# Gate and up of two feed-forwards: part of the K tiles as 2x2 block products with seven multiplications

## The chip, the cores and the metric

The kernel runs on one core of a Trainium2 chip. Its engines work side by side, each through its own queue of instructions in order: TensorE (PE, matrix products into PSUM; the loading of its stationary operand is shown as PEld), VectorE (DVE), ScalarE (ACT), GpSimd (POOL) and SyncE (SP, which issues the loads). They wait for each other through semaphores. The metric is the device time of one execution in microseconds. The kernel before takes 2145.21 us, the median of three runs (2145.0 to 2145.99). By 0.2% of it, 4.3 us, a difference between two kernels can just be told from none.

## The reference

One layer of a Conformer-like encoder on 256 tokens of 2048 features, all in float32. It opens and closes with a feed-forward whose hidden width is 5632:

```python
def swiglu_ffn(h, w_in, w_out):
    gate, up = jnp.split(h @ w_in, 2, axis=-1)
    return (jax.nn.silu(gate) * up) @ w_out

x = x + 0.5 * swiglu_ffn(rms_norm(x, ffn1_norm), ffn1_w_in, ffn1_w_out)
...   # token mixing (convolution and spatial gating), then cross-attention into 256 memory tokens
x = x + 0.5 * swiglu_ffn(rms_norm(x, ffn2_norm), ffn2_w_in, ffn2_w_out)
return rms_norm(x, final_norm)
```

The change is in the two feed-forwards, above all in `h @ w_in`.

## The kernel before

All products are made from two-part numbers. A float32 operand is split into a high part that TensorE takes as it is and the low rest; a product is high x high, high x low and low x high, three matmuls. The weights are split on the way in: SP loads 512 KB into one of four `raw` buffers (L104), ScalarE casts it to the high part (L107), VectorE subtracts that from the raw values (L108) and so gives the low part. High and low part lie in one of three `hl` buffers.

Gate and up (`swiglu_in`) go through 11 groups of 512 hidden columns. In a group the 16 K tiles of 128 features come one after the other; a `raw` tile holds 512 gate and 512 up columns of one K tile. `by_two` makes the products: for each half of the tokens (128 of them, the stationary operand `x_hl`) and for gate and up, three 128x512 matmuls (L273, L274, L277), 12 for a K tile and 192 for a group, summed in four banks of PSUM (`acc`, from a pool of six). Then ScalarE makes silu of gate out of PSUM (L289), VectorE multiplies it by up (L290), and the result `h` waits in one of two buffers. It has tokens on its partitions; the next product needs features there. So `turn` transposes it on TensorE, four 128x128 blocks to a turning (L303), into one of two more banks (`aux`), from where ScalarE and VectorE split it into `hA` or `hB` (L115, L116). The two turnings of a group are made inside the next group, after its fourth and sixth K tile.

The output product (`gemm_n`, L166 to L168) runs over 44 hidden tiles for each of four blocks of 512 columns, two hidden tiles to a load and a step of 12 matmuls.

Work that belongs to other things is put in small parts beside the products: `put` enters parts with a cost, `beside` takes them out by a budget at each step. In the first feed-forward these are four loads of mem and their squares, with a budget of 1.4 in each step; in the second they are the 32 turnings of x (L790), with a budget of 0.4. The order of each engine's queue within all this is set by the tile framework's scheduler. The large operands of two parts (`x_hl`, `hA`, `m_hl`, `y_hl`, `o_hl`) share two big buffers that change hands; a new owner waits until the last reader of the old one is done.

Of the kernel before, what the change touches and what calls it, by code (L numbers as in the profile page):

```python
# [11 lines left out]
F32 = mybir.dt.float32  # L12
# [5 lines left out]
P = 128  # L18
D = 2048
T = 256  # L20
# [15 lines left out]

PV_SIZES = [
# [24 lines left out]
def layer(ctx: ExitStack, tc: tile.TileContext, a: dict):  # L62
# [4 lines left out]
    big = ctx.enter_context(tc.tile_pool(name="big", bufs=2))  # L67
# [170 lines left out]
    def gained_tile(norm):  # L238

        return big.tile([P, KD, 2, T], F32R, name="x_hl", tag="S")  # L240
# [26 lines left out]
    def by_two(acc, x, hi, lo, first, last):  # L267

        for t in range(2):
            s = slice(t * P, (t + 1) * P)  # L270
            for g in range(2):
                c = slice(g * G, (g + 1) * G)
                nc.tensor.matmul(acc[t][g], lhsT=x[:, 0, s], rhs=hi[:, c], start=first, stop=False)  # L273
                nc.tensor.matmul(acc[t][g], lhsT=x[:, 0, s], rhs=lo[:, c], start=False, stop=False)  # L274
            for g in range(2):
                c = slice(g * G, (g + 1) * G)
                nc.tensor.matmul(acc[t][g], lhsT=x[:, 1, s], rhs=hi[:, c], start=False, stop=last)  # L277

    def token_accs():
        return [[ps.tile([P, 2, 256], F32, name="acc").rearrange("p a b -> p (a b)") for _ in range(2)] for _ in range(2)]  # L280

    def swiglu_in(pool, x_hl, root, w_in, hA, hB, first, per):

        turns = []

        def gated(acc, r):
            h = pool.tile([P, 2, G], F32, name="h", bufs=2)
            for t in range(2):
                nc.scalar.activation(out=h[:, t], in_=acc[t][0], func=AF.Silu, scale=r[:, t:t + 1])  # L289
                nc.vector.scalar_tensor_tensor(  # L290
                    out=h[:, t], in0=acc[t][1], scalar=r[:, t:t + 1], in1=h[:, t], op0=ALU.mult, op1=ALU.mult
                )
            return h

        def turn(j, h, half):
            def go():
                f = 4 * j + 2 * half
                dst = hA[:, f:f + 2] if f < KD else hB[:, f - KD:f - KD + 2]
                tp = pa.tile([P, 2, T], F32, name="aux")
                for k in range(2):  # L300
                    for t in range(2):
                        c = slice((2 * half + k) * P, (2 * half + k + 1) * P)
                        nc.tensor.transpose(out=tp[:, k, t * P:(t + 1) * P], in_=h[:, t, c], identity=ident)  # L303
                split(dst[:, :, 0], dst[:, :, 1], tp)
            return go

        r = None
        for j in range(NG):
            if j == 0 and first is not None:
                acc = first()  # L310
            else:
                acc = token_accs()
                for k in range(KD):
                    hi, lo = weights(w_in[j, :, k:k + 1], 1, 2 * G)
                    by_two(acc, x_hl[:, k], hi[:, 0], lo[:, 0], k == 0, k == KD - 1)
                    if k in (3, 5) and turns:
                        turns.pop(0)()
                    beside(per)
            if r is None:
                r = root()  # L320
            h = gated(acc, r)
            turns += [turn(j, h, half) for half in range(2)]
        return turns

    def h_of(hA, hB):
        return lambda k: hA[:, k] if k < KD else hB[:, k - KD]


    x_hl = gained_tile("ffn1_norm")
    ss = st.tile([P, T], F32, name="ss", bufs=2)  # L330

# [604 lines left out]
```

## Time and profile before

| | |
|---|---|
| median of three runs | 2145.21 us |
| the profiled execution | 2147.76 us, its span 2146.0 us |
| PE busy | 2124.5 us, 99% of the span, 9944 matmuls |
| VectorE busy | 1284.9 us, 60% |
| ScalarE busy | 1005.5 us, 47% |
| DMA | 190 GB/s from HBM on average, median landing time of a gate and up load 3.7 us |
| granted TensorE clock | 0.999 |

The busy time of PE is modelled from the pipelined matmuls: a 128x512 matmul is shown with some 0.39 us, though the next one starts earlier. What a matmul costs is therefore read from the spacing of the work that hangs on it, not from its length. The same holds, to a lesser degree, for VectorE, whose instructions overlap a little when they stand back to back. A busy share is an average over stages: the first and last feed-forward, two thirds of the time, are unlike the middle, where VectorE is at 70 to 90% in places.

### The profile page before, as it was taken

How to read it: one execution, taken by the hardware profiler on the slowest of the kernel's cores; microseconds unless marked ns; L12 is line 12 of the kernel's file. 1: busy time of each engine (PE TensorE's matmuls, PEld its weight loads, DVE VectorE, ACT ScalarE, POOL GpSimd, SP SyncE). 2: the span in 40 equal slices, each digit the busy share in tenths (PEclk: the TensorE clock that was granted, in tenths of full speed). 3: DMA queues.
4: the chain of work that ended last, by engine and by line, in shares of the span. 5: the costliest groups of instructions: out<-in, count | busy, mean ns of one | idle time of the engine just before them, and what ended most of it. 6: DMA issues, size and time to landing. Idle time of an engine off the chain costs nothing.

```text
span 2146.0 us, 26016 instructions
## 1 busy us (share of the span) xinstructions
PE 2124.5 (99%) x9944; PEld 1770.8 (83%) x9944; DVE 1284.9 (60%) x1627; ACT 1005.5 (47%) x1234; POOL 13.3 (1%) x23
## 2 busy tenths in 40 slices
PE   8999999999999999999999999999999999999998
PEld 6788888888888888888888888888888888888886
DVE  4655445545554589889877666766644455444444
ACT  5544444444444454544665454544444444444443
POOL 0000000000000000000000000000000000000000
PEclk9999999999999999999999999999999999999999
DMA  7666666666666676656565543666666666666664
GB/s 271 223 189 192 188 189 192 187 188 189 193 188 194 195 245 199 187 177 186 175 199 187 185 158 115 201 193 188 187 189 193 188 186 192 190 208 194 195 191 154
DMA packets 113598, 409.80 MB, mean 191 GB/s; under 512 B 12737, under 2 KB 12865, under 8 KB 113345
## 3 DMA queue, kind: packets, MB, share of 16 engines
q1 hardware_dynamic: 113184, 407.35, 62.2%
q8 instruction: 78, 1.28, 0.2%
q10 hardware_dynamic: 288, 0.79, 0.1%
q14 instruction: 48, 0.39, 0.0%
HBM read 405.99 MB, written 2.10 MB: 190 GB/s over the span
## 4 chain that ended last, share of the span: by engine, by line
PE 95%; DMA 2%; DVE 1%; ACT 1%; issue 1%; SPq 0%; DVEq 0%; ACTq 0%
PE acc L274 14%; PE acc L277 14%; PE acc L273 14%; PE acc L167 12%; PE acc L168 12%; PE acc L166 12%; PE acc L120 8%; PE acc L121 4%; PE acc L857 1%; PE acc L859 1%; PE acc L858 1%; DMA raw<-in_x 1%; PE aux L303 1%; DMA raw<-in_memT 1%; PE aux L257 0%
## 5 line engine op out<-in xcount | busy, mean ns | idle before, releaser
L108 DVE TENSOR_TENSOR hl<-raw,hl 128x1024 fp32r<-128x1024 f32 x751 | 915.6, 1222 | 783.8 <-ACT hl L107 782.4
L107 ACT CAST hl<-raw 128x1024 fp32r<-128x1024 f32 x751 | 784.8, 1049 | 1007.7 <-PE acc L277 505.6
L274 PE MATMUL acc<-hl,x_hl 128*128 128x512 f32 x1408 | 446.9, 392 | 0.6 <-DVE hl L108 0.5
L277 PE MATMUL acc<-hl,x_hl 128*128 128x512 f32 x1408 | 441.3, 390 | 0.0
L273 PE MATMUL acc<-hl,x_hl 128*128 128x512 f32 x1408 | 395.4, 393 | 10.0 <-ACT hl L107 8.4
L273 PEld LDWEIGHTS acc<-hl,x_hl 128*128 128x128 f32 x1408 | 261.5, 188 | 63.5 <-ACT hl L107 9.7
L277 PEld LDWEIGHTS acc<-hl,x_hl 128*128 128x128 f32 x1408 | 264.8, 188 | 55.7
L274 PEld LDWEIGHTS acc<-hl,x_hl 128*128 128x128 f32 x1408 | 263.0, 188 | 55.4 <-DVE hl L108 2.1
L167 PE MATMUL acc<-hl,hB 128*128 128x512 f32 x392 | 152.7, 389 | 0.0
L168 PE MATMUL acc<-hl,hB 128*128 128x512 f32 x392 | 152.6, 389 | 0.0
L166 PE MATMUL acc<-hl,hB 128*128 128x512 f32 x392 | 136.7, 389 | 0.0
L167 PE MATMUL acc<-hl,x_hl 128*128 128x512 f32 x256 | 100.6, 393 | 0.8 <-DVE hl L108 0.8
L167 PE MATMUL acc<-hl,m_hl 128*128 128x512 f32 x256 | 100.4, 392 | 0.0
L168 PE MATMUL acc<-hl,m_hl 128*128 128x512 f32 x256 | 100.2, 392 | 0.0
L168 PE MATMUL acc<-hl,x_hl 128*128 128x512 f32 x256 | 99.8, 390 | 0.0
L166 PE MATMUL acc<-hl,m_hl 128*128 128x512 f32 x256 | 91.3, 393 | 0.0
L120 PE MATMUL acc<-x_hl,hl 128*128 128x512 f32 x256 | 90.6, 396 | 0.0
L120 PE MATMUL acc<-y_hl,hl 128*128 128x512 f32 x256 | 90.5, 399 | 0.0
L166 PE MATMUL acc<-hl,x_hl 128*128 128x512 f32 x256 | 90.2, 392 | 0.0
L120 PE MATMUL acc<-o_hl,hl 128*128 128x512 f32 x256 | 89.2, 393 | 0.0
L167 PE MATMUL acc<-hl,hA 128*128 128x512 f32 x224 | 87.8, 392 | 0.0
L168 PE MATMUL acc<-hl,hA 128*128 128x512 f32 x224 | 87.3, 390 | 0.0
(208 smaller groups left out, 2243.6 us busy)
## 6 DMA issues: line engine op xcount, KB each, us to landing
raw<-in_ffn_w_in SPq DMA_DIRECT2D x352, 512.0 KB, 3.7
raw<-in_ffn_w_out SPq DMA_DIRECT2D x176, 512.0 KB, 3.7
raw<-in_w_mix_vg SPq DMA_DIRECT2D x32, 512.0 KB, 4.5
raw<-in_w_k SPq DMA_DIRECT2D x32, 512.0 KB, 3.8
raw<-in_w_v SPq DMA_DIRECT2D x32, 512.0 KB, 4.2
raw<-in_w_mix_out SPq DMA_DIRECT2D x32, 512.0 KB, 4.5
raw<-in_w_q SPq DMA_DIRECT2D x32, 512.0 KB, 4.3
raw<-in_w_o SPq DMA_DIRECT2D x29, 512.0 KB, 4.5
```

What stands on the lines that cost most here:

```text
L107: nc.scalar.copy(out=hl[:, 0, :size], in_=raw[:, :size])
L108: newest[0] = nc.vector.tensor_tensor(out=hl[:, 1, :size], in0=raw[:, :size], in1=hl[:, 0, :size].bitcast(F32), op=ALU.subtract)
L120: nc.tensor.matmul(acc, lhsT=w_hi, rhs=x_hl, start=first, stop=False, skip_group_check=True)
L121: nc.tensor.matmul(acc[:, 0], lhsT=w_lo, rhs=x_hl[:, 0], start=False, stop=last, skip_group_check=True)
L166: nc.tensor.matmul(acc[t], lhsT=x[:, 0, s], rhs=hi[:, k], start=k0 + k == 0, stop=False)
L167: nc.tensor.matmul(acc[t], lhsT=x[:, 0, s], rhs=lo[:, k], start=False, stop=False)
L168: nc.tensor.matmul(acc[t], lhsT=x[:, 1, s], rhs=hi[:, k], start=False, stop=k0 + k == nk - 1)
L273: nc.tensor.matmul(acc[t][g], lhsT=x[:, 0, s], rhs=hi[:, c], start=first, stop=False)
L274: nc.tensor.matmul(acc[t][g], lhsT=x[:, 0, s], rhs=lo[:, c], start=False, stop=False)
L277: nc.tensor.matmul(acc[t][g], lhsT=x[:, 1, s], rhs=hi[:, c], start=False, stop=last)
L303: nc.tensor.transpose(out=tp[:, k, t * P:(t + 1) * P], in_=h[:, t, c], identity=ident)
L857: nc.tensor.matmul(acc[t], lhsT=x[:, 0], rhs=hi[:, k], start=first, stop=False)
```

## The change

For some pairs of K tiles the 24 matmuls become 21. A pair is taken as a 2x2 block product: the left matrix has the two halves of the tokens as block rows and the two K tiles as block columns, the right one has the two K tiles as block rows and gate and up as block columns. Such a product can be made with seven block multiplications instead of eight, if sums and differences of blocks are multiplied and the results are added afterwards (`seven`). A string says for each of the 8 pairs whether it is done with seven products (S) or as before with eight (C): SCSCSCCC in the first feed-forward, SCCSCCCC in the second. The first group of each feed-forward is done wholly as before.

What comes with it:

- The sums of the left blocks (`sides`, four forms of 128x128 for each S pair) are made once, in the first group, and kept split in `ring`.
- The sums of the right blocks are made by VectorE for each S pair of each group: four instructions of 512 columns (L370, L371, L376, L383). Two of them overwrite part of the raw tile. With them an S pair has three and a half 1024 wide tiles to split instead of two.
- A group uses all eight banks, the two of `aux` included. After its last S pair, ScalarE copies one bank (L418) and VectorE makes four sums (L419 to L422); at the end of the group four more (L432), then silu and the product (L397, L399) from SBUF.
- Since `aux` is taken, h is kept for all 11 groups, and its turnings stand in the last group (four of 22) and in the first output product (18, one after each step).
- The split weights have five buffers instead of three: `hl` and two in `ring`. There are now three big buffers S0, S1, S2; in the middle part `kT` and `vv` lie in one of them.
- The loads of mem and their squares move from the second group to the second and later output products of the first feed-forward, with a budget of 0.8 per step; the 32 turnings of x move into the first group of the second feed-forward, with a budget of 1.3.
- At the end, one `held` buffer is left of four for the last weights; the others come from `hl`.

The right operand is laid out in DRAM so that for even K tiles up stands before gate. That is part of the arrays' preparation. The diff, cut to its core:

```diff
+PATTERNS = ("SCSCSCCC", "SCCSCCCC")
...
-    big = ctx.enter_context(tc.tile_pool(name="big", bufs=2))
+    big = ctx.enter_context(tc.tile_pool(name="big", bufs=1))
...
+    def three(acc, x, hi, lo, first, last):
+
+        nc.tensor.matmul(acc, lhsT=x[0], rhs=hi, start=first, stop=False)
+        nc.tensor.matmul(acc, lhsT=x[0], rhs=lo, start=False, stop=False)
+        nc.tensor.matmul(acc, lhsT=x[1], rhs=hi, start=False, stop=last)
...
+        def parts(self, raw, n=1024, last=False):
+
+            i = self.at % 5
+            self.at += 1
+            hl = whl.tile([P, 2, 1024], F32R, name="hl") if last or i < 3 else self.ring[i - 3]
+            nc.scalar.copy(out=hl[:, 0, :n], in_=raw[:, :n])
+            newest[0] = nc.vector.tensor_tensor(
+                out=hl[:, 1, :n], in0=raw[:, :n], in1=hl[:, 0, :n].bitcast(F32), op=ALU.subtract
+            )
+            return hl
...
+        def seven(self, j, p, b, first, last):
+
+            k = 2 * p
+            one, two = self.raw(j, k), self.raw(j, k + 1)
+            sums = self.sums[self.spairs.index(p) % 2]
+            lo, hi = slice(0, G), slice(G, 2 * G)
+            nc.vector.tensor_tensor(out=sums[:, lo], in0=one[:, hi], in1=one[:, lo], op=ALU.subtract)
+            nc.vector.tensor_tensor(out=sums[:, hi], in0=two[:, hi], in1=one[:, lo], op=ALU.subtract)
+            w = self.parts(sums)
+            form = [(self.forms[self.spairs.index(p)][:, f, 0], self.forms[self.spairs.index(p)][:, f, 1]) for f in range(4)]
+            three(b["5"], form[0], w[:, 0, lo], w[:, 1, lo], first, last)
+            three(b["7"], form[2], w[:, 0, hi], w[:, 1, hi], first, last)
+            nc.vector.tensor_tensor(out=one[:, lo], in0=sums[:, lo], in1=two[:, hi], op=ALU.add)
+            w = self.parts(one)
+            three(b["6"], form[1], w[:, 0, lo], w[:, 1, lo], first, last)
+            three(b["1"], self.x(k, 0), w[:, 0, hi], w[:, 1, hi], first, last)
+            w = self.parts(two)
+            three(b["2"], self.x(k + 1, 0), w[:, 0, lo], w[:, 1, lo], first, False)
+            three(b["3"], form[3], w[:, 0, hi], w[:, 1, hi], first, False)
+            nc.vector.tensor_tensor(out=two[:, lo], in0=two[:, lo], in1=one[:, lo], op=ALU.subtract)
+            w = self.parts(two, G)
+            three(b["4"], self.x(k + 1, 1), w[:, 0, lo], w[:, 1, lo], first, False)
...
+        def group(self, j, r, per, after=()):
...
+            for p, c in enumerate(self.pattern):
+                if c == "S":
+                    self.seven(j, p, b, p == 0, p == self.spairs[-1])
+                    if p == self.spairs[-1]:
+                        nc.scalar.copy(out=p1, in_=b["1"])
+                        nc.vector.tensor_tensor(out=u2, in0=p1, in1=b["6"], op=ALU.add)
+                        nc.vector.tensor_tensor(out=u4, in0=u2, in1=b["5"], op=ALU.add)
+                        nc.vector.tensor_tensor(out=u2, in0=u2, in1=b["7"], op=ALU.add)
+                        nc.vector.tensor_tensor(out=u5, in0=u2, in1=b["5"], op=ALU.add)
+                else:
...
+                beside(per)
+            for acc, u in (("2", p1), ("4", u2), ("3", u4), ("8", u5)):
+                nc.vector.tensor_tensor(out=u, in0=u, in1=b[acc], op=ALU.add)
+            self.give(j, (p1, u2), (u4, u5), r)
...
         for n in range(4):
-            acc = gemm_n(a["ffn1_w_out"][n], h_of(hA, hB), between=turns)
+            acc = gemm_n(a["ffn1_w_out"][n], ff.of, per=0.8 if n else 0.0, between=turns, after=0 if n == 0 else 4)
...
+        def first_beside(k):
+            if 4 <= k < 4 + len(ff.spairs):
+                ff.sides(k - 4)
+            beside(1.3)
...
-            acc_0 = gemm_n(a["ffn2_w_out"][0], h, between=turns)
+        acc_0 = gemm_n(a["ffn2_w_out"][0], h, between=turns, after=0)
```

Three places show what this makes of the engines' order. The first is VectorE in a gate and up group of the first feed-forward. Before, a group is the low parts of its 16 tiles (L108), with the two turnings of the group ahead among them; the middle of one reads:

```order
L290 SCALAR_TENSOR_TENSOR h_789<-acc_448,r_x2_93,h_789 128x512
L108 TENSOR_TENSOR hl_834<-raw_832,hl_834 128x1024
L108 TENSOR_TENSOR hl_851<-raw_849,hl_851 128x1024
L108 TENSOR_TENSOR hl_875<-raw_873,hl_875 128x1024
L108 TENSOR_TENSOR hl_892<-raw_890,hl_892 128x1024
L116 TENSOR_TENSOR hA_97<-aux_866,hA_97 128x2x256
L116 TENSOR_TENSOR hA_97<-aux_907,hA_97 128x2x256
```

The change, from the first use of the second raw tile of an S pair (`raw_866`) to its last:

```order
L371 TENSOR_TENSOR spare_115<-raw_866,raw_864 128x512
L376 TENSOR_TENSOR raw_864<-spare_115,raw_866 128x512
L334 TENSOR_TENSOR ring_114<-spare_115,ring_114 128x1024
L334 TENSOR_TENSOR hl_879<-raw_864,hl_879 128x1024
L334 TENSOR_TENSOR hl_888<-raw_866,hl_888 128x1024
L334 TENSOR_TENSOR ring_114<-raw_904,ring_114 128x1024
L383 TENSOR_TENSOR raw_866<-raw_866,raw_864 128x512
L334 TENSOR_TENSOR ring_114<-raw_920,ring_114 128x1024
L334 TENSOR_TENSOR hl_898<-raw_866,hl_898 128x512
```

Where a raw tile was read by one VectorE instruction, `raw_866` is now held over nine, two of which (of `raw_904` and `raw_920`) belong to the C pair behind it.

The second place is the end of such a group on VectorE, with the first S pair of the next (`raw_792` and `raw_794` are its tiles, `acc_482` to `acc_485` the banks of the group that ends):

```order
L376 TENSOR_TENSOR raw_792<-spare_115,raw_794 128x512
L334 TENSOR_TENSOR ring_114<-spare_115,ring_114 128x1024
L334 TENSOR_TENSOR ring_114<-raw_792,ring_114 128x1024
L334 TENSOR_TENSOR hl_815<-raw_794,hl_815 128x1024
L383 TENSOR_TENSOR raw_794<-raw_794,raw_792 128x512
L432 TENSOR_TENSOR spare_115<-spare_115,acc_482 128x512
L432 TENSOR_TENSOR spare_115<-spare_115,acc_483 128x512
L334 TENSOR_TENSOR hl_825<-raw_794,hl_825 128x512
L432 TENSOR_TENSOR spare_115<-spare_115,acc_484 128x512
L432 TENSOR_TENSOR spare_115<-spare_115,acc_485 128x512
L399 SCALAR_TENSOR_TENSOR h1_104<-spare_115,r_x2_92,h1_104 128x512
L334 TENSOR_TENSOR hl_833<-raw_831,hl_833 128x1024
```

Three of the next group's parts stand ahead of the four closing sums, its fourth between them and its first C tile behind them. Before, nothing but L290 stood there.

The third place is VectorE at the entry of the second feed-forward. Before, the turnings of x (L790) come one at a time between the low parts:

```order
L245 SCALAR_TENSOR_TENSOR xT<-acc,xT 128x256 x2
L790 STREAM_TRANSPOSE x_10903<-xT 32x16x32 x2
L108 TENSOR_TENSOR hl<-raw,hl 128x1024
L790 STREAM_TRANSPOSE x_10903<-xT 32x16x32
L234 SCALAR_TENSOR_TENSOR x_hl<-xT,pv,x_hl 128x256
L210 TENSOR_TENSOR ss<-ss,sq 128x256
L108 TENSOR_TENSOR hl<-raw,hl 128x1024 x2
```

The change (here L951) has them at one to three for each low part, with the sums of the left blocks (L353) among them:

```order
L951 STREAM_TRANSPOSE spare<-xT 32x16x32 x3
L334 TENSOR_TENSOR hl<-raw,hl 128x1024
L951 STREAM_TRANSPOSE spare<-xT 32x16x32 x2
L353 SCALAR_TENSOR_TENSOR spare<-spare 128x128
L334 TENSOR_TENSOR hl<-raw,hl 128x1024
L951 STREAM_TRANSPOSE spare<-xT 32x16x32
L353 SCALAR_TENSOR_TENSOR spare<-spare 128x128
L951 STREAM_TRANSPOSE spare<-xT 32x16x32
L334 TENSOR_TENSOR ring<-raw,ring 128x1024
L951 STREAM_TRANSPOSE spare<-xT 32x16x32 x2
```

All 32 stand ahead of the first S pair; before, they went on into the third group.

256 lines of the change are left out of this document (170 added, 86 removed).

## Prediction

> **What bounds the kernel now.** I read the page's engine table first, then its costliest groups, then the gate and up groups of the first feed-forward as one stretch of time, and then single instructions.
>
> ```profile
> span 2146.0 us, 26016 instructions
> PE 2124.5 (99%) x9944; PEld 1770.8 (83%) x9944; DVE 1284.9 (60%) x1627; ACT 1005.5 (47%) x1234; POOL 13.3 (1%) x23
> ```
>
> ```profile
> 103.00:503.00 400.00, 400.00 (x1802) 330.88 (x1801) 199.81 (x185) 172.27 (x182) 0.00 (x0) 1.00 0.63 189
> ```
>
> ```profile
> L107 ACT CAST hl<-raw 128x1024 fp32r<-128x1024 f32 x745 | 781.2, 1052 | 999.6 <-PE acc L277 505.6 <-PE acc L168 324.4 <-PE acc L121 52.2
> ```
>
> The second row is a window: its span, then the busy time of PE, PEld, DVE, ACT, POOL, granted clock, DMA share and GB/s. The third is a group of instructions: busy time, mean ns, and the idle time before them with what ended it. In those 400 us, which hold groups 2 to 10 of gate and up, PE has no gap at all, while DVE works half of the time. ScalarE's casts wait for matmuls (505.6 us behind L277), not the other way round: the buffers of split weights are always full. So here each matmul taken out of the stream is worth its spacing, until another engine or the loads cannot keep up.
>
> ```profile
> 299.58 1.22 DVE L108 TENSOR_TENSOR hl<-raw,hl 128x1024 fp32r<-128x1024 f32 x1 [1.49 <-ACT hl L107]
> ...
> 302.30 1.23 DVE L108 TENSOR_TENSOR hl<-raw,hl 128x1024 fp32r<-128x1024 f32 x1 [1.50 <-ACT hl L107]
> ...
> 305.02 1.23 DVE L108 TENSOR_TENSOR hl<-raw,hl 128x1024 fp32r<-128x1024 f32 x1 [1.50 <-ACT hl L107]
> ```
>
> One K tile, 12 matmuls, passes every 2.72 us, so a 128x512 matmul costs 0.2267 us of PE. The window agrees: 400.0 / 9 = 44.4 us for a group, of which 192 x 0.2267 = 43.5 are products, and the other 0.9 are two turnings of four transposes, 0.46 us each.
>
> **Term 1, the matmuls removed.** A pair of K tiles done with seven products takes 7 x 3 = 21 matmuls instead of 24. Ten groups of each feed-forward (all but the first) do it, for 3 pairs in the first and 2 in the second: 10 x 3 x 3 + 10 x 2 x 3 = 150 matmuls, 150 x 0.2267 = **-34.0 us**. The order of the changed program has the seven products as plain 128x512 matmuls, so their price is the same.
>
> **What VectorE has to do for it.** The durations must be the ones it has when instructions stand back to back, so I looked where it is crowded.
>
> ```profile
> 1011.02 0.68 DVE L613 TENSOR_TENSOR z<-z,aux 128x512 f32<-128x512 f32 x1
> 1011.62 0.47 DVE L448 SCALAR_TENSOR_TENSOR half<-pad,pv,half 128x256 f32<-128x256 f32 x1
> 1012.01 1.22 DVE L108 TENSOR_TENSOR hl<-raw,hl 128x1024 fp32r<-128x1024 f32 x1
> 1013.15 0.47 DVE L448 SCALAR_TENSOR_TENSOR y<-pad,pv,y 128x256 f32<-128x256 f32 x1
> ```
>
> A 1024 wide two-tensor instruction takes 1.22 us but the next begins 1.14 us after it; a 512 wide one, here with an operand in PSUM, takes 0.68 and the next begins after 0.60. Where the next needs the result it waits for the whole 0.68 and some 0.03. A seven-product pair ("S") costs three low parts of 1024 and one of 512, and four sums of 512: 3 x 1.14 + 5 x 0.60 = 6.4 us, while its 21 matmuls take 4.8. An ordinary pair ("C") costs 2.3 of VectorE against 5.4 of PE. The eight sums from PSUM and two gating products of a group come to about 6.6 us. So a group of SCSCSCCC loads VectorE with 3 x 6.4 + 5 x 2.3 + 6.6 = 37.3 us against 183 x 0.2267 = 41.5 of PE, and one of SCCSCCCC with 12.8 + 13.8 + 6.6 = 33.2 against 42.2. On average PE stays the bound; inside the group it may not.
>
> The Trainium skill (VectorE: DVE Perf Modes, "The DRAIN you can't avoid") says that the next instruction does not start until the pipe of the one before is empty. By that rule one would add up whole durations, 3 x 7.1 + 5 x 2.4 + 7.0 = 40.3 us, nearly PE's 41.5; the trace denies it, 1013.15 being before 1012.01 + 1.22.
>
> **Term 2, the loads in the first feed-forward.** The nearest limit is the four buffers of raw weights. An S pair reads two, and the second one is freed only by its last VectorE instruction. By VectorE's order, shown above with the change, between the first use of the second tile (L371) and its last (the 512 wide L334) stand two dependent sums (0.72 each, and 0.39 more until the cast of the sums, 1.05 us and its hand-overs, is done), four low parts of 1024, the difference L383, one more low part, and the 512 one: 0.72 + 1.11 + 4 x 1.14 + 0.60 + 1.14 + 0.69 = 8.8 us. Then the buffer is loaded again.
>
> ```profile
> raw<-in_ffn_w_in SPq DMA_DIRECT2D x352, 512.0 KB, 3.7
> ...
> raw<-in_w_mix_out SPq DMA_DIRECT2D x32, 512.0 KB, 4.5
> ```
>
> ```profile
> 47.26 5.07 DMA raw<-in_memT
> ```
>
> Median landing is 3.7 us for these weights and 4.5 for another stage's equally large ones. A group has 16 loads and there are four buffers, so the same buffer always serves as the second tile, and the loop from S to the next S is 8.8 + 3.7 = 12.5 us, or 13.3. PE needs 45 x 0.2267 = 10.2 us for S and C. Twice in a group of SCSCSCCC the next S comes after one C: 2 x 2.3 = 4.6 us late, or 2 x 3.1 = 6.2. Against it stands a lead: the three wide parts of a group's first S are made before the closing sums of the group ahead, six products, 18 x 0.2267 = 4.1 us in hand. What is left is 0.5 us a group with the one landing and 2.1 with the other. I take the middle, 1.3, since an S asks for its two tiles almost together: 10 x 1.3 = **+13 us**. The ends: nothing, if VectorE and the loads overlap better than this, and 43 us in the worst case (last rival).
>
> In the second feed-forward two C lie between the S, 69 x 0.2267 = 15.6 us of PE against a loop of 13.3 at most: **0**, covered by PE's own work on two C.
>
> **The closing sums, a wait that is added.** Four sums of each group (L432) wait for its last matmuls, and VectorE's next work is queued behind them, which PE waits for. After the last matmul come at most 2 x 0.60 + 0.69 us until the next group's fourth part is ready, and PE has 4.1 us in hand; then 2 x 0.60 + 0.69 + 1.14 = 3.0 until the first part of its C, 4.9 against 4.8. **0**, with up to 0.5 us a group, +10, as the upper end; no gain is possible here.
>
> **Term 3, the turnings.** h is now kept whole for all eleven groups, and 18 of 22 turnings of each feed-forward move into the first output product (before, 2 did), one after each step of two K tiles.
>
> ```profile
> L116 DVE TENSOR_TENSOR hB<-aux,hB 128x512 fp32r<-128x512 f32 x28 | 18.1, 682 | 0.0
> L115 ACT CAST hB<-aux 128x512 fp32r<-128x512 f32 x28 | 15.1, 585 | 0.0
> ```
>
> PE pays 0.46 us for each wherever it stands. A step then has 2.72 + 0.46 = 3.2 us of PE over 1.14 + 0.60 of VectorE and 1.05 + 0.59 of ScalarE, and each turning stands four steps ahead of its use: **0**, covered by the product's matmuls; 2 us either way.
>
> **Term 4, the entry of the second feed-forward.** All 32 turnings of x now fall into its first group; before they were spread over about three.
>
> ```profile
> L790 DVE STREAM_TRANSPOSE x<-xT 32x512 f32<-32x512 f32 x32 | 22.5, 703 | 1.0
> L290 DVE SCALAR_TENSOR_TENSOR h<-acc,r_x,h 128x512 f32<-128x512 f32 x44 | 32.8, 750 | 4.8 <-ACT h L289 4.8
> ```
>
> VectorE then has 16 x 1.14 + 32 x 0.70 + 2 x 0.75 = 42.1 us, and for the left sides of two pairs at most 2 x (4 x 0.42 + 0.68) = 4.7, up to the end of the first group, and 6.4 for the first S: 53.2, while PE has 43.5 + 4.8 = 48.3. The sides' instructions are narrower than the rows I price them by, the transposes can overlap, and a little of the S may be made early. So I take **+3 us** of the 4.9; ends 0 and 8 (a landing behind it).
>
> **Term 5, the start.** The four loads of mem and their squares leave group 1 and go beside the later output products.
>
> ```profile
> 56.90:103.10 46.20, 43.90 (x195) 35.19 (x194) 27.61 (x35) 24.57 (x34) 0.00 (x0) 1.00 0.73 237
> ```
>
> ```profile
> 56.89 1.28 ACT L289
> ...
> 65.25 6.31 DMA raw<-in_ffn_w_in
> ```
>
> ```profile
> L210 DVE TENSOR_TENSOR sm<-sm,sq 128x256 f32<-128x256 f32 x15 | 6.3, 421 | 0.6
> ```
>
> Group 1 takes 46.2 us instead of 44.4: it waits for the table load and gate values at 56.89, which hold the banks it needs, and for a load that took 6.31 us among those of mem. Its S starts in banks that are free, so up to 1.8 us and as much at the end of group 0 can come back; against it stand the left sides of three pairs and the first S, which has no lead. **-2 us**, between -4 and +4. Where the squares go, one load is added to about two steps; a step there has 2.72 us of PE over 1.14 + 4 x 0.42 = 2.8 on VectorE, spread over two steps: 0, a microsecond either way.
>
> **The sum.** The profiled execution took 2147.8 us (2146.0 of span and 1.8 around it): 2147.8 - 34.0 + 13 + 3 - 2 = 2127.8. It stands 2.5 above the median of the runs, 2145.2, so the forecast is 2125.
>
> **The rivals.** (a) The loads are hidden after all: no stall in the groups, 2125.3 - 13 = 2112. For it speaks that VectorE has 4 us of slack in a group; against it that the reload loop is longer than S and C by the rows. The Trainium skill (DMA: Bandwidth & Descriptors, "Anatomy of one DMA — SWDGE (gpsimd) path") puts such a transfer at 2.0 us + bytes / 436 GB/s, an estimate of 3.2 us; by it the loop is 12.0 and the lead covers it, which is this rival. The row of 3.7 denies it for this queue. (b) The closing sums stall each of 20 boundaries by 0.5 us: 2125 + 10 = 2135. (c) The loop is slower because VectorE's instructions cost their whole durations: the hold is 9.3, with 4.5 of landing 13.8, and 2 x 3.6 - 4.1 = 3.1 us are lost per group: 2125.3 - 13 + 31 = 2143, no change that can be told; it is what the rule on the DRAIN, named above, would make of it. (d) The change loses: the same loop with a landing of 5.07, as the load of mem had when several stood in the queue: 14.4, and 2 x 4.2 - 4.1 = 4.3 us per group: 2125.3 - 13 + 43 = 2155. This decides once the ten groups of the first feed-forward lose more than 3.7 us each (34.0 - 3 + 2 + 4.3, over ten). For it speaks that each S asks for two tiles at once; against it that DMA is busy only 0.63 of the time in the window above.
>
> **How the numbers follow.** Chances: my forecast 0.53, (a) 0.12, (b) 0.07, (c) 0.12, (d) 0.16. Within 0.2% (4.3 us, about what this measurement can tell from no change) is (c) alone, slower is (d), the rest is faster: 0.72, 0.12, 0.16. The range leaves out the lowest part of (a) and most of (d): 2110 to 2150.
>
> **What would show it.** The profile after should have 9794 matmuls, 1050 of them on L272 to L274; groups of the first feed-forward every 42 to 44 us and of the second every 42.2; VectorE's busy time up by some 345 us (50 pairs x 4.7 and 20 groups x 8 x 0.69), ScalarE's idle time before casts of hl no longer put down to PE alone. Small PE waits on L272 and L285 to L288 inside the first feed-forward, released by ScalarE or VectorE behind a DMA, would be term 2; none of them is (a); waits at the first matmuls of every group are (b); DMA landings of 5 us and waits of over 3.7 us a group are (d). The forecast is wrong if the second feed-forward stalls in its groups too, since I cost it at nothing.

## The result, and the profile after

The changed kernel takes 2138.72 us, the median of six runs (2136.46 to 2142.93), beside 2145.99 for the kernel before on the same chip (six runs). The ratio is 0.9969, with a 95% interval of 0.9956 to 0.9981: faster by 7.3 us, where 20 had been forecast. The profiled execution took 2141.02 us, 2139.2 of them span.

First the page of the changed kernel: span, engines, the chain of waits by engine, and the median landing time of the gate and up loads.

```profile
span 2139.2 us, 26365 instructions
...
PE 2103.8 (98%) x9794; PEld 1742.7 (81%) x9794; DVE 1588.1 (74%) x2112; ACT 1090.4 (51%) x1367; POOL 13.3 (1%) x23
...
PE 78%; DVE 10%; DMA 7%; ACT 2%; issue 2%; SPq 0%; ACTq 0%; DVEq 0%
...
raw<-in_ffn_w_in SPq DMA_DIRECT2D x352, 512.0 KB, 4.6
```

The 150 matmuls are gone, but 17% of the chain that ended last now runs over VectorE and DMA, where it was 3% before. To see where, take eight groups of each feed-forward, groups 2 to 9. Each window below is as long as the stretch from the first matmul of group 2 to that of group 10, and its ends lie within 0.4 us of them. Windows of the changed kernel (columns as in the prediction):

```profile
101.66:449.19 347.53, 340.14 (x1466) 273.32 (x1465) 301.09 (x351) 179.91 (x200) 0.00 (x0) 1.00 0.59 194
1500.18:1837.46 337.28, 337.28 (x1490) 279.40 (x1489) 270.28 (x304) 171.33 (x185) 0.00 (x0) 1.00 0.63 199
```

Eight groups of 183 matmuls should take 8 x 183 x 0.2267 = 331.9 us; they take 347.5, 2.0 more per group. Eight of 186 should take 337.3 and take exactly that. So the pattern SCCSCCCC runs without a gap, and SCSCSCCC does not. Groups 1 and 10 of the first feed-forward lose time too: group 1 takes 47.5 us for 41.5 us of work, group 10 some 2.3 us more than its 43.3 (41.5 and four turnings).

Stage by stage, against the kernel before (all read from the first matmul of each stage): gate and up of the first feed-forward end 9.4 us earlier, but its first output product takes 7.5 more, since the turnings stand there now. After it only 1.9 us are left of the 20.4 that 90 matmuls are worth, and 1.4 of them are lost again before the second feed-forward starts. That one gains the rest of the 6.8 us by which the span is shorter.

The waits in the first window, by the engine that waits (us in total, times, longest):

```profile
ACT hl L333 <- DVE spare L371: 33.0, 8, 6.5
ACT ring L333 <- DVE spare L371: 28.8, 7, 5.1
...
DVE spare L371 <- DMA raw<-in_ffn_w_in: 16.9, 18, 2.0
...
DVE spare L370 <- DMA raw<-in_ffn_w_in: 10.0, 8, 3.4
```

ScalarE waits for the sums of an S pair, the sums for the load of its raw tiles. One such place in VectorE's order, an S at 325.7 and the next one at 337.9:

```profile
325.74 0.68 DVE L371 TENSOR_TENSOR spare<-raw 128x512 f32<-128x512 f32 x1
...
331.02 1.22 DVE L334 TENSOR_TENSOR ring<-raw,ring 128x1024 fp32r<-128x1024 f32 x1
332.16 0.68 DVE L383 TENSOR_TENSOR raw<-raw 128x512 f32<-128x512 f32 x1
332.76 1.22 DVE L334 TENSOR_TENSOR ring<-raw,ring 128x1024 fp32r<-128x1024 f32 x1
333.90 0.68 DVE L334 TENSOR_TENSOR hl<-raw,hl 128x512 fp32r<-128x512 f32 x1
337.95 0.69 DVE L370 TENSOR_TENSOR spare<-raw 128x512 f32<-128x512 f32 x1 [3.37 <-DMA raw<-in_ffn_w_in]
339.22 0.69 DVE L371 TENSOR_TENSOR spare<-raw 128x512 f32<-128x512 f32 x1 [0.58 <-DMA raw<-in_ffn_w_in]
```

The loop is as the prediction had it, a pair that waits for its tiles to be loaded again, and here L371 returns after 13.5 us where S and C have 10.2 us of PE. Its inside is different. The chain of waits there:

```profile
332.16 0.69 DVE raw L383
332.85 0.02 issue
332.87 6.33 DMA raw<-in_ffn_w_in
339.20 0.02 issue
339.22 0.70 DVE spare L371
```

The second tile's load goes into the buffer that L383 frees, the first raw tile of the S ahead, 7.1 us after L371 and not 8.8; but it lands 6.33 us later, not 3.7 or 4.5. This is the longest of nine such loops. In groups 2 to 10, L371 of the third S follows that of the second after 10.3 to 13.5 us, 11.6 in the median: 6.6 until the second tile's load is issued and 4.5 until it lands. Between the first and the second S, where the closing sums stand in VectorE's queue, it is 13.2 us, but there the lead covers most of it. Of the 15.6 us that the eight groups lose, some 11 stand at the third S, 4.7 of them at this one place (a wait of PE and a slower clock after it; see the last section).

A landing is longer than before because loads stand together in SP's queue, here that of the changed kernel and then of the kernel before in the same stretch:

```profile
332.27 2.77 SPq L341 DMA_DIRECT2D raw<-in_ffn_w_in  x4
```

```profile
332.79 10.14 SPq L104 DMA_DIRECT2D raw<-in_ffn_w_in  x5
```

Before, a load is issued every 2.5 us or so, and lands 3.6 us later in the median of groups 2 to 9. Now all four buffers come free at the end of VectorE's block of work on an S pair (the two low parts of the C, L383, the 512 wide low part), and four loads go out within 2.8 us. Groups 2 to 10 have 18 such fours; their loads land 3.7, 4.4, 5.4 and 5.6 us after their issue in the median, the first to the fourth. Those shown took 5.65, 6.33, 6.44 and 7.10: here even the first is late, and why is not shown. The four issued from 345.76 on took 3.73 to 5.33.

### The profile page after: what moved, and what is told of

Same layout as the page of the kernel before. It is cut to its first block, busy times and chain, and to the rows that moved or that the text cites. A ratio compares the mean times of both kernels' runs of the same rounds, so it can differ in the third digit from the quotient of the medians.

```text
span 2139.2 us, 26365 instructions
## 1 busy us (share of the span) xinstructions
PE 2103.8 (98%) x9794; PEld 1742.7 (81%) x9794; DVE 1588.1 (74%) x2112; ACT 1090.4 (51%) x1367; POOL 13.3 (1%) x23
## 3 DMA queue, kind: packets, MB, share of 16 engines
q8 instruction: 76, 1.25, 0.2%
## 4 chain that ended last, share of the span: by engine, by line
PE 78%; DVE 10%; DMA 7%; ACT 2%; issue 2%; SPq 0%; ACTq 0%; DVEq 0%
PE acc L170 12%; PE acc L171 12%; PE acc L169 12%; PE acc L123 8%; PE acc L286 6%; PE acc L285 6%; PE acc L288 6%; DMA raw<-in_ffn_w_in 6%; PE acc L124 4%; DVE hl L334 3%; DVE ring L334 2%; PE acc L274 2%; PE acc L273 2%; PE acc L272 1%; PE aux L260 1%
## 5 line engine op out<-in xcount | busy, mean ns | idle before, releaser
L111 DVE TENSOR_TENSOR hl<-raw,hl 128x1024 fp32r<-128x1024 f32 (+1 forms) x402 | 489.8, 1219 | 326.3 <-ACT hl L110 325.3
L110 ACT CAST hl<-raw 128x1024 fp32r<-128x1024 f32 (+1 forms) x402 | 419.7, 1045 | 486.1 <-PE acc L171 296.1
L333 ACT CAST hl<-raw 128x1024 fp32r<-128x1024 f32 (+1 forms) x249 | 244.7, 1001 | 153.8 <-DMA raw<-in_ffn_w_in 73.3
L334 DVE TENSOR_TENSOR hl<-raw,hl 128x1024 fp32r<-128x1024 f32 (+1 forms) x249 | 285.0, 1160 | 38.9 <-ACT hl L333 37.2
L286 PE MATMUL acc<-hl,x_hl 128*128 128x512 f32 x620 | 211.0, 392 | 1.1 <-DVE hl L334 1.0
L285 PE MATMUL acc<-hl,x_hl 128*128 128x512 f32 x620 | 197.9, 392 | 7.0 <-ACT hl L333 7.0
L333 ACT CAST ring<-raw 128x1024 fp32r<-128x1024 f32 (+1 forms) x153 | 149.6, 988 | 106.3 <-DMA raw<-in_ffn_w_in 54.0
L288 PE MATMUL acc<-hl,x_hl 128*128 128x512 f32 x620 | 193.3, 390 | 0.0
L334 DVE TENSOR_TENSOR ring<-raw,ring 128x1024 fp32r<-128x1024 f32 (+1 forms) x153 | 173.1, 1143 | 21.6 <-ACT ring L333 21.2
L285 PEld LDWEIGHTS acc<-hl,x_hl 128*128 128x128 f32 x620 | 116.9, 189 | 31.8 <-ACT hl L333 7.5
L286 PE MATMUL acc<-ring,x_hl 128*128 128x512 f32 x388 | 137.1, 392 | 3.0 <-DVE ring L334 3.0
L286 PEld LDWEIGHTS acc<-hl,x_hl 128*128 128x128 f32 x620 | 116.0, 189 | 27.3 <-DVE hl L334 3.7
L288 PEld LDWEIGHTS acc<-hl,x_hl 128*128 128x128 f32 x620 | 116.7, 188 | 24.5
L285 PE MATMUL acc<-ring,x_hl 128*128 128x512 f32 x388 | 129.4, 390 | 0.6 <-ACT ring L333 0.6
L288 PE MATMUL acc<-ring,x_hl 128*128 128x512 f32 x388 | 122.1, 390 | 0.0
L170 PE MATMUL acc<-hl,x_hl 128*128 128x512 f32 x256 | 100.6, 393 | 0.3 <-DVE hl L111 0.3
L171 PE MATMUL acc<-hl,x_hl 128*128 128x512 f32 x256 | 99.8, 390 | 0.0
```

The source lines that it names most:

```text
L110: nc.scalar.copy(out=hl[:, 0, :size], in_=raw[:, :size])
L111: newest[0] = nc.vector.tensor_tensor(out=hl[:, 1, :size], in0=raw[:, :size], in1=hl[:, 0, :size].bitcast(F32), op=ALU.subtract)
L170: nc.tensor.matmul(acc[t], lhsT=x[:, 0, s], rhs=lo[:, k], start=False, stop=False)
L171: nc.tensor.matmul(acc[t], lhsT=x[:, 1, s], rhs=hi[:, k], start=False, stop=k0 + k == nk - 1)
L285: nc.tensor.matmul(acc[t][g], lhsT=x[:, 0, s], rhs=hi[:, cols[g]], start=(t, g) in first, stop=False)
L286: nc.tensor.matmul(acc[t][g], lhsT=x[:, 0, s], rhs=lo[:, cols[g]], start=False, stop=False)
```

## The experiments

**Eight raw buffers in the first feed-forward.** Four more, in the half of the spare buffer that only the second feed-forward uses.

```diff
+            self.extra = 4 if gain == "ffn1_norm" else 0
+            self.x2_raw = [spare[:, i * 1024:(i + 1) * 1024] for i in range(self.extra)]
...
-            raw = wraw.tile([P, 1024], F32, name="raw")
+            i = self.loads % (4 + self.extra)
+            self.loads += 1
+            raw = wraw.tile([P, 1024], F32, name="raw") if i < 4 else self.x2_raw[i - 4]
```

> Four more raw buffers in the first feed-forward (eight instead of four, in a part of a buffer that lies idle there); everything else as in the changed kernel. Theory L (reload loop): the 17.5 us that groups 2 to 10 of the first feed-forward lose over 41.5 us each (with 1.8 for the four turnings of the last) come from raw tiles that an S pair holds too long and that must be loaded again; with eight buffers a load stands a whole S and C ahead, groups 2 to 9 take 41.5 to 41.9, no wait of VectorE's L370 or L371 on a DMA is left there, and the time falls by 15 to 18 us, to 2121 to 2125. Theory V (VectorE's own order is late, or the closing sums are): the loads were only the last to come, the stalls stay within 4 us of what they were, 2135 to 2140.

2117.42 us, ratio 0.9867 (0.9853 to 0.9882). The same eight groups, as a window of this kernel:

```profile
95.49:427.33 331.84, 331.84 (x1466) 274.77 (x1465) 299.17 (x354) 181.55 (x201) 0.00 (x0) 1.00 0.63 203
```

331.84 us: no gap, with the same work on VectorE (299 us against 301). Theory V falls. The landings did not get shorter (4.5 and 4.7 us in the median for the two sorts of buffers), so it is the return of the buffers that cost time, and a longer landing costs nothing where enough of them are there. The time fell by more than expected, 21.3 us, because group 1 takes 42.6 us instead of 47.5.

That part is another wait. Its largest piece in the changed kernel is a wait of PE for a bank that silu of group 0's gate must free:

```profile
60.83 0.50 PE L272 MATMUL acc<-ring,x_hl 128*128 128x512 f32 x1 [2.94 <-ACT h L397]
```

The scale r_x that silu needs was ready at 53.5 us. But in ScalarE's queue silu stands behind the last cast of the S and a table load:

```profile
58.16 0.62 ACT L333 CAST ring<-raw 128x512 fp32r<-128x512 f32 x1 [2.46 <-DVE raw L383]
58.80 1.28 ACT L397 ACT_TABLE_LOAD   x1
60.09 1.26 ACT L397 ACTIVATE h<-acc,r_x 128x512 f32<-128x512 f32 x2
```

With five, six or eight buffers the scheduler put the table load ahead of that cast; with six:

```profile
51.71 1.28 ACT L402 ACT_TABLE_LOAD   x1 [2.44 <-DVE r_x L205]
53.01 0.69 ACT L402 ACTIVATE h<-acc,r_x 128x512 f32<-128x512 f32 x1
```

How much of group 1's 6.0 us is this order, and how much its loads, was not separated.

**The dose: five and six buffers.** The same edit with one and with two tiles more.

> Two more raw buffers in the first feed-forward (six), else the changed kernel. Theory L with two tiles held: with six, an S is loaded into tiles that the C ahead of the S before it used, and the two tiles of an S are next needed only by a C, S + C + S = 15.0 us of PE after the S, against a hold of 8.8 and a landing of 4.6 to 5.1; nothing is late, groups 2 to 9 take 41.5, the time is that of eight buffers, 2117.4, within 2 us. If instead each buffer more only adds some slack to a loop of any length (landing times that scatter), six lie between four and eight: 2121 to 2130.

> One more raw buffer in the first feed-forward (five). Theory L: the second tile of an S now waits for the first tile of the S before it, which is free after L383, some 0.7 to 1.7 us before the other one, and the first tile of an S waits for a C. The loop is still longer than the 10.2 us of S and C: a stall is left, at L371 and no more at L370, between a third and two thirds of that with four buffers: 2122 to 2131. If the stall came from the first tile alone, five would do: 2117 to 2119. If it came from the number of loads that stand in the queue together, one buffer more would not help: 2136 to 2141.

Six: 2117.21 us, ratio 0.9863 (0.9848 to 0.9878), the time of eight, as theory L had it. Five: 2134.17 us, 0.9941 (0.9926 to 0.9956), a miss. Windows of the eight groups, with six and then with five:

```profile
94.66:426.50 331.84, 331.84 (x1465) 274.78 (x1464) 301.07 (x354) 182.40 (x202) 0.00 (x0) 1.00 0.65 203
```

```profile
94.93:443.25 348.32, 337.95 (x1466) 272.74 (x1465) 303.70 (x355) 180.39 (x200) 0.00 (x0) 1.00 0.60 193
```

With five the groups lose as much as with four (348.3 against 347.5 us); the 4.5 us came from group 1 (41.9 us), so of the 21.5 us that six buffers bring, about that much is group 1 and not the loop. I had expected the wait to move to the second tile. It moved the other way:

```profile
DVE spare L375 <- DMA raw<-in_ffn_w_in: 19.3, 15, 2.7
...
DVE spare L376 <- DMA raw<-in_ffn_w_in: 5.4, 8, 1.0
```

(L375 and L376 are L370 and L371 there.) The fifth buffer was used up by a longer burst: around 253 us five loads are issued within 5.2 us and land 5.7 to 6.7 us later. So the step from five to six is not gradual. The account in the expectation for six, that an S's two tiles then reuse those of a C that is long done, is counted from the order of the loads and not read from the trace. Why five bring nothing in the groups stays open.

**The hold shortened instead.** Four buffers, but the difference goes to its own tile, early.

```diff
+            diff = self.own.tile([P, G], F32, name="diff", bufs=2)
+            nc.vector.tensor_tensor(out=diff, in0=two[:, lo], in1=one[:, lo], op=ALU.subtract)
...
-            nc.vector.tensor_tensor(out=two[:, lo], in0=two[:, lo], in1=one[:, lo], op=ALU.subtract)
-            w = self.parts(two, G)
+            w = self.parts(diff, G)
```

> Four raw buffers as in the changed kernel, but the difference L383 is written to a tile of its own right after L376, so that both raw tiles of an S pair are free after their low parts and not only after the 512 wide one. VectorE has exactly the same instructions. Theory L: the hold falls from 8.8 us to about 0.6 + 0.72 + 0.69 + 3 x 1.14 = 5.4, with a landing of 4.6 to 5.1 the loop is 10.0 to 10.5 against 10.2 of PE; nearly all of the 17.5 us goes: 2122 to 2126. Theory V: the same VectorE work, the same stalls, 2136 to 2141.

2129.24 us, ratio 0.9923 (0.9908 to 0.9938): 9.5 us of the 21.5, more than theory V allows and less than theory L promised. Its eight groups:

```profile
100.67:438.46 337.79, 333.69 (x1466) 274.25 (x1465) 302.42 (x355) 182.11 (x200) 0.00 (x0) 1.00 0.63 200
```

15.6 us of loss became 5.9, with the same instructions on VectorE, one of them earlier and into another tile. Group 1 kept its loss (47.7 us).

**Two S in the first feed-forward.**

```diff
-PATTERNS = ("SCSCSCCC", "SCCSCCCC")
+PATTERNS = ("SCCSCCCC", "SCCSCCCC")
```

> The first feed-forward as SCCSCCCC, the second one's pattern. 30 matmuls more, +6.8 us. Theory L: with two C between the S the loop is covered as it is in the second feed-forward, whose groups 3 to 9 take their 42.16 exactly; the 17.5 us go: 2139 + 6.8 - 17.5 = 2128, 2126 to 2131. Theory C (closing sums, L432, stall every boundary in the first feed-forward): the stalls stay, 2143 to 2148.

2128.96 us, ratio 0.9919 (0.9902 to 0.9935), as theory L had it. 30 matmuls more and 9.8 us less time; groups 2 to 9 take 42.16 us each in both feed-forwards. Group 1 kept its loss here too (47.9 us). Closing sums that stall every boundary are excluded by this and by the runs with six and eight buffers.

**The entry of the second feed-forward: x turned more slowly.**

```diff
-            beside(1.3)
+            beside(0.4)
```

> The 32 turnings of x in the second feed-forward with a budget of 0.4 instead of 1.3 per step, so that they spread over some five groups. Theory E (VectorE is full in the first group): the first two groups of the second feed-forward, which lose 4.5 and 2.7 us, lose 1 to 2 together, and the time falls by 4 to 6 us, to 2133 to 2136. Theory F (the first S of the second group, which has no lead, and the gate values of the first group, for which its banks wait, are the loss): it falls by less than 2 us, 2137 to 2140; and the turnings beside S pairs could cost up to as much again.

2136.97 us, ratio 0.9963 (0.9948 to 0.9978): 1.8 us, in F's range, and hardly more than two measurements of one program differ by (1.6 us, below). First the changed kernel, groups 0 and 1 of the second feed-forward as windows, then this one (group 1 of the changed kernel ends at 1500.18, after 44.9 us):

```profile
1407.30:1455.30 48.00, 46.08 (x198) 35.91 (x196) 46.94 (x69) 20.42 (x25) 0.00 (x0) 1.00 0.54 163
1455.30:1500.00 44.70, 42.55 (x187) 34.69 (x186) 36.14 (x42) 24.92 (x27) 0.00 (x0) 1.00 0.61 192
```

```profile
1409.60:1453.50 43.90, 43.90 (x198) 36.42 (x196) 36.16 (x49) 20.63 (x26) 0.00 (x0) 1.00 0.60 187
1453.50:1501.00 47.50, 44.09 (x189) 36.02 (x189) 36.88 (x45) 24.95 (x27) 0.00 (x0) 0.96 0.56 174
```

The place in this run's second group where PE waits longest:

```profile
1459.99 0.50 PE L272 MATMUL acc<-ring,x_hl 128*128 128x512 f32 x1 [3.40 <-ACT h L397]
```

In this profile both theories are right, one for each group. VectorE was busy 46.94 of 48.00 us in group 0; with the turnings spread, PE has no gap there. But the next thing was right behind it: group 1's products wait 3.40 us for banks that silu of group 0 must free (L397), and silu starts at 1459.25, behind VectorE's last piece of r_x2 at 1459.01. The profiled execution took 2142.2 us, the longest of its four, so group 1's loss may be smaller in the others.

**And r_x2 asked for early.**

```diff
+            if k == 1:
+                x_r.append(rms_cols(ss, D, "r_x2"))
...
-        turns = ff.run(lambda k: None, first_beside, lambda: rms_cols(ss, D, "r_x2"), 0.4)
+        turns = ff.run(lambda k: None, first_beside, lambda: x_r[0], 0.4)
```

> As the run with the turnings of x at a budget of 0.4, and the reciprocal root of the second feed-forward's sum of squares (r_x2, seven short instructions and a table load) is asked for in the second step of the first group instead of at its end. In that run the first group lost 0.4 us and the second 5.4, with a gap of 3.4 us that ended with silu of the first group's gate, behind VectorE's last piece of r_x and a table load. Theory G (the gate waits for r_x): the gap goes, with the slow matmuls behind it, the second group loses 1 to 2 us, and the time falls by 3.5 to 4.5 us against that run, to 2132 to 2134. Theory F (the first S has no lead and its banks wait for the first group's gate however early r_x is): less than 1.5 us, 2135.5 to 2138.

2131.18 us, ratio 0.9927 (0.9911 to 0.9944), 5.8 us below the run before it; theory G had 3.5 to 4.5. Both groups run through:

```profile
1404.60:1448.60 44.00, 44.00 (x198) 36.54 (x197) 37.57 (x54) 23.81 (x30) 0.00 (x0) 1.00 0.58 184
1448.60:1490.70 42.10, 42.10 (x188) 34.85 (x187) 36.04 (x42) 21.94 (x24) 0.00 (x0) 1.00 0.63 201
```

**r_x2 early alone**, the turnings left at 1.3.

> The changed kernel with r_x2 of the second feed-forward asked for in the second step of its first group, and the turnings of x left at a budget of 1.3 as in the changed kernel. In the changed kernel the first two groups lose 4.5 and 2.7 us; with the turnings spread alone 0.4 and 5.4; with both edits 0.5 and 0. Theory E+G (two separate losses: VectorE full in the first group, the gate late in the second): the first group still loses 4 to 5, the second up to 1.5: 2135.5 to 2138. Theory G alone (the late gate behind all of it): both go, as with both edits: 2131 to 2133.

2140.31 us, ratio 0.9971 (0.9959 to 0.9982), a miss for both theories: the changed kernel's time. It tells nothing about the gate, because the edit left the order of every instruction of PE, VectorE and ScalarE as it was, so it is the changed kernel measured once more, with a median 1.6 us away. Among turnings that fill VectorE the scheduler puts the pieces of r_x2 at the same places, the first one 26 us into the group and the last one 49 us. The two rows are from this run.

```profile
1433.47 0.16 DVE L200 TENSOR_SCALAR rv<-aux 128x2 f32<-128x2 f32 x1
...
1455.82 0.15 DVE L205 SCALAR_TENSOR_TENSOR r_x<-rt,r_x 128x2 f32<-128x2 f32 x1
```

How much of the 2.7 us of group 1 in the changed kernel is the gate and how much VectorE's backlog stays open; that both edits together remove all of it is seen in their profile.

**All together.** Eight buffers and SCSCSCCC in both feed-forwards, r_x2 early, x turned beside the first output product of the second:

```diff
+PATTERNS = ("SCSCSCCC", "SCSCSCCC")
...
+            self.extra = 4
...
+        put(0.6, *[turn(i, j) for i in range(4) for j in range(8)])
+        acc_0 = gemm_n(a["ffn2_w_out"][0], h, per=1.2, between=turns, after=0)
+        finish()
```

> All that the theories say together: eight raw buffers in both feed-forwards, SCSCSCCC in both, r_x2 early, and the 32 turnings of x of the second feed-forward beside its first output product, where a step of 3.2 us of PE stands over 1.7 of VectorE. Against the run with eight buffers in the first feed-forward (2117.4): 30 matmuls fewer, -6.8; the entry of the second feed-forward, which loses 7 us there, -4 to -6; the turnings in the output product 0, up to +3. Theory L: 2105, 2103 to 2110. If VectorE is the limit of SCSCSCCC once x is turned elsewhere, or the output product stalls under 50 us of VectorE's work in 70: 2112 to 2120.

2106.7 us (2103.81 to 2110.59), ratio 0.9814 (0.9799 to 0.9829), as expected: the fastest of these kernels, 32 us below the changed one. The second feed-forward's entry, as windows:

```profile
1380.69:1424.69 44.00, 44.00 (x199) 36.50 (x198) 32.28 (x50) 25.05 (x33) 0.00 (x0) 1.00 0.68 233
1424.69:1466.17 41.48, 41.48 (x185) 34.36 (x184) 36.20 (x42) 23.18 (x26) 0.00 (x0) 1.00 0.64 199
```

**A fourth S.** The same with SCSCSCSC in groups 1 to 9.

```diff
-PATTERNS = ("SCSCSCCC", "SCSCSCCC")
+PATTERNS = ("SCSCSCSC", "SCSCSCSC")
...
+                    self.pattern, self.spairs = "SCSCSCCC", [0, 2, 4]
```

> The fastest kernel so far (eight raw buffers and SCSCSCCC in both feed-forwards, r_x2 early, x turned in the output product; 2106.7) with SCSCSCSC in groups 1 to 9 of both, the last group as before: 54 matmuls fewer, -12.2 if nothing waits. VectorE then is the test: priced by its starts, 4 x 6.4 + 4 x 2.3 + 6.6 = 41.4 us a group against 40.8 of PE, some 41.5, so no gain and no loss within 8: 2100 to 2115. Priced by whole durations (the rival with the DRAIN) it is 4 x 7.1 + 4 x 2.4 + 7.0 = 45.0, 3.5 more than now in 18 groups: 2165 to 2172. If VectorE's order adds waits of its own where it is full, between the two, and VectorE would show idle time in the groups: 2115 to 2165.

2190.27 us, ratio 1.0198 (1.0181 to 1.0215): slower than all three cases. A window of this kernel in the first feed-forward:

```profile
150.00:450.00 300.00, 284.21 (x1164) 218.10 (x1162) 265.01 (x319) 154.45 (x174) 0.00 (x0) 0.98 0.56 180
```

The nine groups of the first feed-forward take 46.1 us on average. VectorE is busy 265 of 300 us, which is 40.7 us a group, about the 41.4 that its starts add up to; whole durations would give 45.0. So its work was priced right, and the loss goes with the 12% in which it waits, for casts, banks and loads. Eight stretches of 3.4 us at half TensorE clock, some 1.7 us each (last section), are a part of it. Which wait comes first was not settled.

## Why the prediction was right or wrong

**Term 1 and the price of VectorE: right.** With six buffers eight groups take 331.84 us, 8 x 183 x 0.2267. VectorE is busy 301.07 / 8 = 37.6 us a group there; 37.3 was the sum made from its starts, 40.3 that from whole durations (rival c). The sign named for it, VectorE's busy time up by some 345 us, was priced by durations after all: it rose by 303, and 50 pairs x 4.1 and 160 sums x 0.60, by starts, are 301. The passage of the Trainium skill on the DRAIN (VectorE: DVE Perf Modes, "The DRAIN you can't avoid"), from which rival (c) was made, adds that a next instruction that is not held starts earlier; these rows agree with that addition, as 331.02 + 1.22 is past 332.16. With VectorE busy for 91% of these groups PE has no gap in them; with a fourth S it has some.

**Term 2, the loads: the largest step that failed, by its size.** The mechanism was named, and the runs with six and eight buffers show it. The failing step is "I take the middle", 1.3 us a group between 0.5 with a landing of 3.7 and 2.1 with 4.5, which gave +13. Groups 2 to 10 lose 17.9 us, 2.0 each. The landing was taken from a kernel whose loads are issued one at a time, while the change itself makes them bunch: VectorE works on an S as one block, and at its end four buffers come free together. The second tile of the third S lands after 4.5 us in the median, the upper of the two values. That the loss comes near its 2.1 is partly luck. The hold is 6.6 and not 8.8, since the second tile takes over the first tile's buffer; the two loops of a group are 13.2 and 11.6 us long, 3.0 and 1.4 over the 10.2 of PE; and with these the prediction's own sum, 3.0 + 1.4 - 4.1, gives 0.3. The rest is in one place of 4.7 us, slow clock included, and in smaller waits elsewhere; that the lead is worth its whole 4.1 us is not shown. The sentence "an S asks for its two tiles almost together" was the right hint, with no price drawn from it. Rival (d) had the right kind of cause, a longer landing in a crowded queue, but its 4.3 us a group was twice the measured. That the second feed-forward loses nothing to it was right.

**The closing sums: right, 0.** **Term 3, the turnings: right, 0.** The first output product, before and then changed:

```profile
503.92:564.72 60.80, 60.80 (x274) 50.30 (x273) 29.57 (x26) 25.70 (x27) 0.00 (x0) 1.00 0.65 191
```

```profile
494.78:563.10 68.32, 68.32 (x338) 56.94 (x337) 42.32 (x50) 36.30 (x50) 0.00 (x0) 1.00 0.58 170
```

16 turnings more, 7.52 us or 0.47 each, and PE has no gap. The groups save as much.

**Term 4, the entry of the second feed-forward: right in kind, too small.** +3 was taken, of ends 0 and 8. The two first groups lose 4.5 and 2.7 us where they lost 0.5 and 0 before: 6.7. The step "the transposes can overlap, and a little of the S may be made early" gave away 2 us that VectorE did not have (it is busy 46.94 of 48.00 us), and the second group was left out: a backlog need not end with the group that makes it, and r_x2, queued on the same engine, can hold the gate that holds the banks. How the 2.7 divides between these two is open.

**Term 5, the start: wrong in the changed kernel.** The prediction's window of group 1 begins 2.5 us late. In the kernel before, its first matmul is this one, and group 2 starts at 103.08:

```profile
54.37 0.50 PE L273 MATMUL acc<-hl,x_hl 128*128 128x512 f32 x1 [0.44 <-ACT hl L107]
```

So group 1 took 48.7 us, 4.3 above its 44.4. In the changed kernel it takes 47.5, 6.0 above its 41.5: +1.7 us and not -2. The wait for the table load and the gate values did not go: the S's last cast now stands ahead of them in ScalarE's queue. With six buffers, and another order there, group 1 takes 41.48 and all of it comes back.

Put into the sum, 2147.8 - 34.0 + 17.9 + 6.7 + 1.7 and the 1.4 lost in the middle, which the prediction did not have, are 2141.5, against 2141.0 measured. So of the 13 us between 2127.8 and the measured time, terms 2, 4 and 5 make 4.9, 3.7 and 3.7; all three erred the same way. What the 1.4 are was not looked into.

Rival (a), the loads hidden, said 2112; with six buffers it is 2117. The estimate of 3.2 us that stands beside it is for transfers that GpSimd issues, as the title of its section says; these are issued by SyncE, and one at a time they landed after 3.6 us.

## What to carry to other kernels

A landing time read from a kernel whose loads are evenly spaced is not the landing time after a change that makes buffers come free in bunches; count how many loads will be issued within one landing, and price the one that the loop waits for. When a stage is given more work on a second engine, the buffers that this engine holds should be counted again before the products are: here two more tiles were worth three times the whole change, some of it because the order of a queue changed with them. And a backlog on an in-order engine can be paid once more by the short instructions that queue in it, such as a scalar that gates the next group.

## What the runs showed of the hardware

In these traces TensorE's clock is halved for 3.41 us at a time, and that can follow a short gap. Windows of the changed kernel around the wait at 338 to 341 us (granted clock in the third column from the right):

```profile
338.00:341.41 3.41, 0.91 (x4) 0.48 (x3) 2.33 (x4) 1.39 (x2) 0.00 (x0) 1.00 0.41 162
341.41:344.82 3.41, 3.41 (x9) 2.18 (x9) 3.41 (x4) 2.50 (x3) 0.00 (x0) 0.50 0.00 0
```

After the gap the clock granted is 0.50, and nine matmuls fit where 15 would at 0.2267 us each. At the matmuls themselves:

```profile
341.12 0.58 PE L272 MATMUL acc<-hl,ring 128*128 128x512 f32 x1 [2.50 <-ACT hl L333]
...
343.09 0.63 PE L273 MATMUL acc<-hl,ring 128*128 128x512 f32 x1
343.51 0.63 PE L274 MATMUL acc<-hl,ring 128*128 128x512 f32 x1
```

They start 0.43 us apart instead of 0.23; 3.41 us at half clock cost 1.7 us on top of the gap. The Trainium skill (TensorE: Matmul & The Clock Gate, "HAM oscillation — how this bites in real kernels") warns of idle gaps over about 3.4 us; here a PE wait of 2.50 us did it. The length of the gap alone does not decide. The first row below is from the run with the turnings of x spread, around a gap of 1.25 us; the other two are from the run with r_x2 early alone, around one of 1.95:

```profile
768.17:771.58 3.41, 1.80 (x7) 0.89 (x6) 1.97 (x4) 3.41 (x8) 0.00 (x0) 1.00 0.03 13
```

```profile
335.94:339.35 3.41, 2.02 (x9) 1.32 (x8) 2.08 (x3) 0.71 (x1) 0.00 (x0) 1.00 0.77 291
339.35:342.77 3.42, 2.81 (x11) 2.03 (x12) 3.05 (x3) 3.42 (x5) 0.00 (x0) 1.00 0.01 4
```

The first was followed by half clock, the second was not. The traces show what the two differ in. Seven of the twelve profiled runs have such stretches before their end, 20 in all. Each lasts 3.41 us, and within a run they begin a whole number of 3.413 us apart (in the changed kernel 82, from 61.51 to 341.41), so the time falls into fixed slots. PE's busy time in one slot goes with the clock of the next. Between 20 and 2095 us, all 16 slots in which PE is shown busy for at most 1.75 us are followed by half clock, as are four of the nine from 1.79 to 1.97, and none above. The gap of 1.95 us lies across the end of a slot, at 339.35, and leaves both above that. So the cost of a wait of two or three microseconds on PE is that wait, and 1.7 us more if most of it falls into one slot.
